# Eight experts on one core: all result stores behind the last weight load, smaller pieces of two weight matrices

## The chip, the cores and the metric

The kernel runs on one core of a Trainium2 chip. The other cores are idle. The metric is the device time of one launch in microseconds (us), as the median of three runs. A profile of one such launch is shorter by a little than the launch's own time, because it begins with the first instruction and ends with the last. Times "at 152.9 us" are counted from the start of that profiled span.

Five engines work side by side on a core: TensorE (PE, matrix products; its weight loads are listed as PEld), VectorE (DVE), ScalarE (ACT), GpSimd (POOL) and SyncE (SP). Data go between the chip's main memory (HBM) and the on-chip buffer (SBUF) by DMA. Three engines issue DMAs in this kernel. POOL issues all loads that convert fp32 to fp16 on the way, and most stores; the profile calls its queue q0. SP (q1) and ACT (q10) issue a few more.

## The reference

There are 8 experts. Each has 256 rows of input, a first layer from 512 to 2048 with a ReLU, and a second layer from 2048 to 512. All arrays are fp32.

```python
n_experts, capacity, hidden, expert_hidden = 8, 256, 512, 2048

def reference(x, w1, w2, b1, b2):
    h = np.matmul(x, w1) + b1[:, np.newaxis, :]
    h = np.maximum(h, 0)
    return (np.matmul(h, w2) + b2[:, np.newaxis, :]).astype(np.float32)
```

For each expert the first weights (w1) and the second weights (w2) are 4 MiB each in HBM, the input x and the result are 512 KiB each. So 8 experts read 64 MiB of weights and 4 MiB of x, and write 4 MiB of results.

## The kernel before

Weights are converted to fp16 while they are loaded, so a weight matrix fills 2 MiB of SBUF. All loads are issued on one queue, in an order that the program fixes (`ordered`). The list `ring` holds these issues, each with the step from which on it may be put out. `first_product(s)` computes the hidden layer of expert s, and `second_product(s - LAG)` the result of the expert three steps behind it.

```python
    LAG = 3
    LATE = (3, 4, 5, 6)
    PARTS = {5: ((0, 25, True), (25, 121, False), (121, 128, False))}
    nXF32 = 2
    ...
    w1_pool  = ... bufs=3
    w2_pool  = ... bufs=3
    w2t_pool = ... bufs=1          # the pieces of w2 of expert 7
    hT_pool  = ... bufs=LAG + 2    # hidden layers, 8 KiB per partition each
    out_pool = ... bufs=5          # results, 4 KiB per partition each
    ...
    def load_w2(e):
        src = w2[e].rearrange("(p j) h -> p j h", j=nJ)      # nJ = 16
        w2_sb[e] = []
        t = w2_pool.tile([P, nJ, H], fp16, tag="w2", name="w2sb")
        step = nJ if e < E - 2 else nJ // 2
        for lo in range(0, nJ, step):
            ordered(nc.gpsimd.dma_start(out=t[:, lo : lo + step, :], in_=src[:, lo : lo + step, :]))
            w2_sb[e].append((lo, lo + step, t[:, lo : lo + step, :]))

    def load_w2_piece(e, lo, hi):
        t = w2t_pool.tile([P, hi - lo, H], fp16, tag=f"w2_{lo}", name=f"w2_{lo}")
        ordered(nc.gpsimd.dma_start(out=t, in_=src[:, lo:hi, :]))
    ...
    def flush(e):                                            # the store of expert e, from POOL
        dst, src = pending.pop(e)
        for p0, p1, sync in PARTS.get(e, ((0, P, False),)):
            if not sync:
                ordered(nc.gpsimd.dma_start(out=dst[p0:p1], in_=src[p0:p1]))

    def store(e, po):
        out_sb = out_pool.tile([P, nTB, H], fp32, tag="out", name="out")
        nc.vector.tensor_copy(out=out_sb[:, 0, :], in_=po[0])
        nc.scalar.copy(out=out_sb[:, 1, :], in_=po[1])
        ...                                                  # e < 7: kept in pending for flush
        else:                                                # expert 7
            nc.sync.dma_start(out=dst[:, 0, :], in_=out_sb[:, 0, :])
            nc.scalar.dma_start(out=dst[:, 1, :], in_=out_sb[:, 1, :])

    def second_product(e):
        po = []
        for tb in range(nTB):                                # bias first
            ...matmul(out=t, lhsT=ones1, rhs=b2_sb[...], start=True, stop=False)
        for lo, hi, t in w2_sb[e]:                           # piece by piece
            for tb in range(nTB):
                for j in range(lo, hi):
                    ...matmul(out=po[tb], lhsT=hT[e][:, j, tb * P : (tb + 1) * P],
                              rhs=t[:, j - lo, :], start=False, stop=(j == nJ - 1))
        store(e, po)

    x32 = singles.tile([P, nXF32, nTB, H], fp32)             # x of experts 0 and 1 as fp32
    ...
    ring = []
    for s in range(1, E + LAG - 1):
        if s < E:
            if s >= nXF32:
                ring.append((s - 2, load_x, (s,)))
            ring.append((s - 2, load_w1, (s,)))
        if s >= LAG:
            ring.append((s - 2, load_w2, (s - LAG,)))
        if s >= 2 * LAG and s - 2 * LAG not in LATE:
            ring.append((s - 2, flush, (s - 2 * LAG,)))      # experts 0, 1, 2
    for lo, hi in ((0, 4), (4, 8), (8, 12), (12, 14), (14, 16)):
        ring.append((0, load_w2_piece, (E - 1, lo, hi)))
    for e in LATE:
        ring.append((e + LAG + 1, flush, (e,)))              # experts 3, 4, 5, 6

    for s in range(E + LAG):
        while ring and ring[0][0] <= s:
            _, put, args = ring.pop(0)
            put(*args)
        if s < E:
            first_product(s)
        if s >= LAG:
            second_product(s - LAG)
```

So the stores of experts 0, 1 and 2 stand among the loads: that of expert 0 between w2 of expert 3 and x of expert 6, that of expert 1 between w2 of expert 4 and w2 of expert 5, that of expert 2 between w2 of expert 5 and w2 of expert 6. The stores of experts 3 to 6 stand behind the last piece of w2 of expert 7. Expert 5's store is cut in three, of 25, 96 and 7 partitions; the first goes out from SP as soon as the result is there.

Of the kernel before, what the change touches and what calls it, by code (L numbers as in the profile page):

```python
# [11 lines left out]
def kernel(  # L12
# [9 lines left out]
    nc = tc.nc  # L22
    fp32 = mybir.dt.float32
    fp16 = mybir.dt.float16
    E, T, H = x.shape
    M = w1.shape[2]
    P = 128
    nTB = T // P
    nKC = H // P
    nJ = M // P  # L30
    LAG = 3
    LATE = (3, 4, 5, 6)

# [1 line left out]
    nXF32 = 2  # L37

    def ordered(ins):
        return tc.keep_in_program_order(ins)  # L40

    singles = ctx.enter_context(tc.tile_pool(name="singles", bufs=1))
# [2 lines left out]
    w2t_pool = ctx.enter_context(tc.tile_pool(name="w2t", bufs=1))  # L45
    x_pool = ctx.enter_context(tc.tile_pool(name="xp", bufs=4))
    xT_pool = ctx.enter_context(tc.tile_pool(name="xTp", bufs=2))
    hT_pool = ctx.enter_context(tc.tile_pool(name="hT", bufs=LAG + 2))
    out_pool = ctx.enter_context(tc.tile_pool(name="outp", bufs=5))
    psum_x = ctx.enter_context(tc.tile_pool(name="psum_x", bufs=1, space=bass.MemoryType.PSUM))  # L50
    psum_h = ctx.enter_context(tc.tile_pool(name="psum_h", bufs=3, space=bass.MemoryType.PSUM))
    psum_o = ctx.enter_context(tc.tile_pool(name="psum_o", bufs=2, space=bass.MemoryType.PSUM))
# [8 lines left out]
    x16 = [None] * E  # L61
# [3 lines left out]
    hT = [None] * E  # L65
# [14 lines left out]
    def load_w2(e):  # L80
        src = w2[e].rearrange("(p j) h -> p j h", j=nJ)
        w2_sb[e] = []
        t = w2_pool.tile([P, nJ, H], fp16, tag="w2", name="w2sb")
        step = nJ if e < E - 2 else nJ // 2
        for lo in range(0, nJ, step):
            ordered(nc.gpsimd.dma_start(out=t[:, lo : lo + step, :], in_=src[:, lo : lo + step, :]))  # L86
            w2_sb[e].append((lo, lo + step, t[:, lo : lo + step, :]))
# [80 lines left out]
                    ))  # L168
        store(e, po)

    x32 = singles.tile([P, nXF32, nTB, H], fp32)
    for e in range(nXF32):
        (nc.sync if e == 0 else nc.scalar).dma_start(out=x32[:, e], max_dma_last_dim=2048, in_=x[e].rearrange("(p tb) h -> p tb h", tb=nTB))
    nc.scalar.dma_start(out=b1_rows, in_=b1.rearrange("e (s i) -> (e s) i", s=2))
    load_w1(0)
    ordered(nc.gpsimd.dma_start(  # L176
        out=b2_sb,
        in_=b2.rearrange("e h -> (e h)").rearrange("(o f) -> o f", o=1),
# [4 lines left out]

    for e in range(nXF32):
        x16[e] = x_pool.tile([P, nTB, H], fp16, tag="x16", name="x16")
        nc.vector.tensor_copy(out=x16[e], in_=x32[:, e])  # L186

    pb = psum_x.tile([P, nJ, E, 2], fp32, tag="psx", name="pb")
    for j in range(nJ):
        for s in range(2):  # L190
            ordered(nc.tensor.matmul(  # L191
                out=pb[s * 64 : (s + 1) * 64, j, :, :],
# [5 lines left out]
    for s in range(2):  # L198
        nc.vector.tensor_copy(  # L199
            out=b1T[s * 64 : (s + 1) * 64, :, :], in_=pb[s * 64 : (s + 1) * 64, :, :, s]  # L200
# [5 lines left out]
# [5 lines that stand above are left out]
            ring.append((s - 2, load_w1, (s,)))  # L211
        if s >= LAG:
            ring.append((s - 2, load_w2, (s - LAG,)))
        if s >= 2 * LAG and s - 2 * LAG not in LATE:
            ring.append((s - 2, flush, (s - 2 * LAG,)))
    for lo, hi in ((0, 4), (4, 8), (8, 12), (12, 14), (14, 16)):
        ring.append((0, load_w2_piece, (E - 1, lo, hi)))
    for e in LATE:
        ring.append((e + LAG + 1, flush, (e,)))
# [40 lines left out]
```

## Time and profile before

| | |
|---|---|
| time, median of 3 runs | 183.32 us (182.97 to 183.61) |
| profiled span | 180.8 us |
| PE busy with matmuls | 138.1 us (76%) |
| ACT busy | 62.7 us (35%) |
| DVE busy | 13.2 us (7%) |
| POOL busy | 20.4 us (11%) |
| read from HBM, written to HBM | 71.39 MB, 4.19 MB |

The page gives busy times of the engines, the same in 40 slices of the span, the DMA queues, the chain of work that ended last, and the groups of instructions. Two things about its DMA figures help to read it. The GB/s of a slice count the bytes on the SBUF side, where a converted weight has half the size that it has in HBM: a store of fp32 results therefore shows about twice the GB/s of a weight load that keeps the DMA engines just as busy. And a DMA's time "from issue to landing" includes the time in which it stands behind earlier DMAs in its queue.

### The profile page before, as it was taken

The numbers are of one execution on the slowest core, as the hardware profiler recorded it, in microseconds if no ns is written. First come the engines' busy times: TensorE is split into PE (matmuls) and PEld (weight loads), VectorE is DVE, ScalarE is ACT, GpSimd is POOL, SyncE is SP. The second block draws the span as 40 slices with busy tenths as digits, with TensorE's granted clock in tenths as the row PEclk, the third lists the DMA queues.
The fourth block names the chain that finished last, engine by engine and source line by source line (L and its number), as shares of the span: only waits on it lengthen the run. The fifth ranks groups of instructions, "written<-read, shape, count | busy, mean of one in ns | idle before, by whom it ended". The sixth has DMA issues, their size and how long they took to land.

```text
span 180.8 us, 2129 instructions
## 1 busy us (share of the span) xinstructions
PE 138.1 (76%) x912; PEld 95.3 (53%) x912; DVE 13.2 (7%) x21; ACT 62.7 (35%) x137; POOL 20.4 (11%) x44
## 2 busy tenths in 40 slices
PE   0555979579550999939993799908999994999991
PEld 0544969469550754836473654807559641334340
DVE  0320001001000101010100101001010010010101
ACT  0022769639570340816044330903309501010101
POOL 7200030300300010210010100200004201112100
PEclk9999999969998599996999789996999999799999
DMA  5989999998999999899989999989998998999996
GB/s 187 281 185 234 232 199 207 204 260 174 234 232 207 199 232 232 177 229 232 225 181 226 238 210 196 228 234 233 232 225 181 290 228 241 223 209 218 213 367 243
DMA packets 5831, 40.58 MB, mean 224 GB/s; under 512 B 670, under 2 KB 686, under 8 KB 3774
## 3 DMA queue, kind: packets, MB, share of 16 engines
q0 software_dynamic: 4928, 38.71, 97.5%
q1 hardware_dynamic: 446, 0.89, 1.4%
q10 hardware_dynamic: 448, 0.85, 1.3%
q8 instruction: 7, 0.11, 0.2%
q14 instruction: 2, 0.02, 0.0%
HBM read 71.39 MB, written 4.19 MB: 418 GB/s over the span
## 4 chain that ended last, share of the span: by engine, by line
DMA 59%; PE 25%; issue 9%; another core or an unknown queue 3%; POOL 2%; ACT 0%; POOLq 0%; ACTq 0%
DMA x<-in_x_dram 25%; DMA w2sb<-in_w_dram 22%; PE po L162 16%; DMA w1sb<-in_w_dram 13%; PE ph L114 7%; PE po L156 1%; PE psx L101 1%; POOL w2sb L86 1%; POOL w1sb L76 1%; ACT out L140 0%; POOL out_dram L135 0%; POOL b_sb L176 0%; POOL ident masks.py:199 0%; POOL ident masks.py:197 0%
## 5 line engine op out<-in xcount | busy, mean ns | idle before, releaser
L114 PE MATMUL ph<-xT,w1sb 128*128 128x256 f16 x512 | 68.4, 300 | 9.8 <-DMA w1sb<-in_w_dram 9.8
L121 ACT ACTIVATE hT<-ph,b1T 128x256 f16<-128x256 f32 x128 | 57.1, 474 | 43.2 <-PE ph L114 42.8
L114 PEld LDWEIGHTS <-w1sb 128*128 128x128 f16 x512 | 61.5, 149 | 16.0 <-DMA w1sb<-in_w_dram 10.8
L162 PE MATMUL po<-w2sb,hT 128*128 128x512 f16 x224 | 51.2, 388 | 2.6 <-DMA w2sb<-in_w_dram 2.6
L162 PEld LDWEIGHTS <-hT 128*128 128x128 f16 x256 | 24.8, 99 | 35.6 <-issue 8.2
L140 ACT COPY out<-po 128x512 f32<-128x512 f32 x8 | 4.7, 588 | 60.6 <-PE po L162 60.6
L101 PE MATMUL psx<-ident,x 128*128 128x128 f16 x64 | 6.2, 254 | 19.7 <-DMA x<-in_x_dram 19.0
L101 PEld LDWEIGHTS <-x 128*128 128x128 f16 x64 | 5.0, 124 | 20.7 <-DMA x<-in_x_dram 19.9
L107 DVE COPY xT<-psx 128x1024 f16<-128x1024 f16 x8 | 5.5, 692 | 81.2 <-PE psx L101 81.2
L76 POOL DMA_DIRECT2D w1sb<-in_w_dram x8 | 4.5, 559 | 61.4 <-PE ph L114 60.6
L139 DVE COPY out<-po 128x512 f32<-128x512 f32 x8 | 5.5, 692 | 73.9 <-PE po L162 73.9
L86 POOL DMA_DIRECT2D w2sb<-in_w_dram x8 | 4.3, 534 | 48.2 <-PE po L162 48.2
L191 PE MATMUL pb<-ident,b_rows 16*64 16x16 f32 x64 | 3.7, 265 | 6.6 <-DMA b_rows<-in_b_dram 6.6
L162 PE MATMUL po<-w,hT 128*128 128x512 f16 x32 | 7.1, 379 | 0.0
L191 PEld LDWEIGHTS pb<-ident,b_rows 16*64 16x64 f32 x64 | 3.6, 198 | 6.5 <-issue 6.5
L135 POOL DMA_DIRECT2D out_dram<-out x8 | 4.3, 535 | 20.7 <-DMA w2sb<-in_w_dram 10.5
L121 ACT ACT_TABLE_LOAD x1 | 1.3, 1283 | 11.0 <-DVE b1T L199 11.0
L156 PE MATMUL po<-b_sb,ones 1*128 1x512 f16 x16 | 4.8, 379 | 0.0
L92 POOL DMA_DIRECT2D w<-in_w_dram x5 | 2.7, 540 | 14.4 <-DMA w2sb<-in_w_dram 13.7
L70 POOL DMA_DIRECT2D x<-in_x_dram x6 | 3.3, 548 | 5.3 <-DMA w2sb<-in_w_dram 4.6
L156 PEld LDWEIGHTS <-ones 1*128 1x128 f16 x16 | 0.9, 92 | 2.1 <-issue 2.1
L186 DVE CAST x<-x 128x1024 f16<-128x1024 f32 x2 | 1.4, 700 | 4.3 <-DMA x<-in_x_dram 4.3
(9 smaller groups left out, 2.6 us busy)
## 6 DMA issues: line engine op xcount, KB each, us to landing
w1sb<-in_w_dram POOLq DMA_DIRECT2D x8, 2048.0 KB, 33.7
w2sb<-in_w_dram POOLq DMA_DIRECT2D x6, 2048.0 KB, 45.3
out_dram<-out POOLq DMA_DIRECT2D x6, 512.0 KB, 30.1
w2sb<-in_w_dram POOLq DMA_DIRECT2D x2, 1024.0 KB, 25.6
x<-in_x_dram POOLq DMA_DIRECT2D x6, 256.0 KB, 38.9
w<-in_w_dram POOLq DMA_DIRECT2D x3, 512.0 KB, 29.7
x<-in_x_dram SPq DMA_DIRECT2D x1, 512.0 KB, 4.5
x<-in_x_dram ACTq DMA_DIRECT2D x1, 512.0 KB, 5.3
```

The source lines that it names most:

```text
L76: ordered(nc.gpsimd.dma_start(out=w1_sb[e], in_=w1[e].rearrange("(p kc) m -> p kc m", kc=nKC)))
L86: ordered(nc.gpsimd.dma_start(out=t[:, lo : lo + step, :], in_=src[:, lo : lo + step, :]))
L101: ordered(nc.tensor.transpose(out=pt[:, kc, tb * P : (tb + 1) * P], in_=x16[e][:, tb, :].rearrange("p (q kc) -> p q kc", kc=nKC)[:, :, kc] ...
L107: nc.vector.tensor_copy(out=xT[e], in_=pt)
L114: ordered(nc.tensor.matmul(out=ph, lhsT=w1_sb[e][:, kc, :].rearrange("p (q j) -> p q j", j=nJ)[:, :, j], rhs=xT[e][:, kc, :], start=(kc == 0),
L121: nc.scalar.activation(out=hT[e][:, j, :], in_=ph, func=mybir.ActivationFunctionType.Relu, bias=b1T[:, j, e : e + 1], scale=1.0,)
L135: ordered(nc.gpsimd.dma_start(out=dst[p0:p1], in_=src[p0:p1]))
L139: nc.vector.tensor_copy(out=out_sb[:, 0, :], in_=po[0])
L140: nc.scalar.copy(out=out_sb[:, 1, :], in_=po[1])
L156: ordered(nc.tensor.matmul(out=t, lhsT=ones1, rhs=b2_sb[0:1, e * H : (e + 1) * H], start=True, stop=False,))
L162: ordered(nc.tensor.matmul(out=po[tb], lhsT=hT[e][:, j, tb * P : (tb + 1) * P], rhs=t[:, j - lo, :], start=False, stop=(j == nJ - 1),))
L191: ordered(nc.tensor.matmul(out=pb[s * 64 : (s + 1) * 64, j, :, :], lhsT=b1_rows.rearrange("r (q j) -> r q j", j=nJ)[:, :, j], rhs=ident[0 ...
```

## The change

All seven stores of experts 0 to 6 are put behind the last load, so that no store stands in front of a weight. For that, all results have to be kept until then: eight result buffers in place of five. The room comes from the fp32 copies of x of experts 0 and 1, which now use two of these eight buffers (they are read once, at the start), and from the hidden layers, of which four are kept in place of five. Two loads are cut otherwise: w2 of expert 5 comes in two halves, so that its product can begin with the first half, and w2 of expert 7 in three pieces of 8, 4 and 4 rows in place of five of 4, 4, 4, 2 and 2.

```diff
-    LATE = (3, 4, 5, 6)
+    LATE = range(E - 1)
...
-    hT_pool = ctx.enter_context(tc.tile_pool(name="hT", bufs=LAG + 2))
-    out_pool = ctx.enter_context(tc.tile_pool(name="outp", bufs=5))
+    hT_pool = ctx.enter_context(tc.tile_pool(name="hT", bufs=LAG + 1))
+    out_pool = ctx.enter_context(tc.tile_pool(name="outp", bufs=E))
...
-        step = nJ if e < E - 2 else nJ // 2
+        step = nJ if e < E - 3 else nJ // 2
...
-    x32 = singles.tile([P, nXF32, nTB, H], fp32)
+    x32 = []
     for e in range(nXF32):
-        (nc.sync if e == 0 else nc.scalar).dma_start(out=x32[:, e], max_dma_last_dim=2048, in_=...)
+        x32.append(out_pool.tile([P, nTB, H], fp32, tag="out", name="x32"))
+        (nc.sync if e == 0 else nc.scalar).dma_start(out=x32[e], max_dma_last_dim=2048, in_=...)
...
-        if s >= 2 * LAG and s - 2 * LAG not in LATE:
-            ring.append((s - 2, flush, (s - 2 * LAG,)))
-    for lo, hi in ((0, 4), (4, 8), (8, 12), (12, 14), (14, 16)):
+    for lo, hi in ((0, 8), (8, 12), (12, 16)):
         ring.append((0, load_w2_piece, (E - 1, lo, hi)))
     for e in LATE:
         ring.append((e + LAG + 1, flush, (e,)))
```

One more thing moves by itself: ACT now issues the load of b1 ahead of its load of x of expert 1, where it was behind it.

More of the change, by code (lines that the diff above doesn't have):

```diff
@@ L169, in second_product @@
         store(e, po)
-    x32 = singles.tile([P, nXF32, nTB, H], fp32)
+    x32 = []
     for e in range(nXF32):
-        (nc.sync if e == 0 else nc.scalar).dma_start(out=x32[:, e], max_dma_last_dim=2048, in_=x[e].rearrange("(p tb) h -> p tb h", tb=nTB))
+        x32.append(out_pool.tile([P, nTB, H], fp32, tag="out", name="x32"))
+        (nc.sync if e == 0 else nc.scalar).dma_start(
+            out=x32[e], max_dma_last_dim=2048, in_=x[e].rearrange("(p tb) h -> p tb h", tb=nTB)
+        )
     nc.scalar.dma_start(out=b1_rows, in_=b1.rearrange("e (s i) -> (e s) i", s=2))
@@ L185 @@
         x16[e] = x_pool.tile([P, nTB, H], fp16, tag="x16", name="x16")
-        nc.vector.tensor_copy(out=x16[e], in_=x32[:, e])
+        nc.vector.tensor_copy(out=x16[e], in_=x32[e])
     pb = psum_x.tile([P, nJ, E, 2], fp32, tag="psx", name="pb")
```

## The prediction

> **What bounds the kernel now.** I read the DMA queues of the page first, because a kernel that moves 75 MB in 180 us is suspect there, then the slices, then the end of the span in short windows, and the chain of waits last.
>
> ```profile
> q0 software_dynamic: 4928, 38.71, 97.5%
> HBM read 71.39 MB, written 4.19 MB: 418 GB/s over the span
> DMA  5989999998999999899989999989998998999996
> GB/s 187 281 185 234 232 199 207 204 260 174 234 232 207 199 232 232 177 229 232 225 181 226 238 210 196 228 234 233 232 225 181 290 228 241 223 209 218 213 367 243
> ```
>
> POOL's queue alone keeps the 16 DMA engines occupied for 97.5% of the span; with q1 (1.4%), q10 (1.3%) and q8 (0.2%) it is 100.4%, so the records of packets overlap by a few per cent and no room is left. The DMA row is 8 or 9 in all slices but the first, some 2 us long at start-up, and the last. A single 8 is the resolution of the slices, since windows cut over the same time show a share of 1.00 or more. The windows are the view that carries the prediction (after the stretch come its length, then PE, PEld, DVE, ACT and POOL busy, the granted PE clock, the DMA share, GB/s on the SBUF side):
>
> ```profile
> 4.00:73.00 69.00, 49.15 (x398) 41.05 (x399) 6.13 (x10) 30.12 (x66) 6.77 (x13) 0.93 1.03 220
> 155.00:171.00 16.00, 16.00 (x71) 6.61 (x70) 1.38 (x2) 1.17 (x2) 2.42 (x5) 0.96 1.03 213
> 172.00:173.00 1.00, 1.00 (x6) 0.48 (x5) 0.00 (x0) 0.00 (x0) 0.00 (x0) 1.00 1.12 272
> 175.00:176.00 1.00, 1.00 (x7) 0.47 (x5) 0.00 (x0) 0.00 (x0) 0.00 (x0) 1.00 1.03 418
> 177.00:178.00 1.00, 0.00 (x0) 0.00 (x0) 0.09 (x1) 0.40 (x1) 0.00 (x0) 1.00 0.70 289
> 178.00:179.00 1.00, 0.00 (x0) 0.00 (x0) 0.00 (x0) 0.00 (x0) 0.00 (x0) 1.00 1.03 387
> 179.00:179.50 0.50, 0.00 (x0) 0.00 (x0) 0.00 (x0) 0.00 (x0) 0.00 (x0) 1.00 0.70 262
> 179.50:180.80 1.30, 0.00 (x0) 0.00 (x0) 0.00 (x0) 0.00 (x0) 0.00 (x0) 0.76 0.00 0
> ```
>
> The rate tells what moves: about 213 GB/s is weights (half size on this side), about 418 GB/s is results. The step between them lies in 172 to 173 us, so the last weight lands near 172.8. The DMA engines are full until 177, are at 0.70 for one microsecond (a loss of 0.30 us), work again until about 179.4, and 1.3 us later the span ends. All idle time that DMA has after the start is thus some 0.3 to 0.45 us at the end.
>
> PE, on the other hand, has slack, and waits for DMA at nearly every expert. Its last stretch:
>
> ```profile
> 122.62 1.04 PE L101 MATMUL psx<-ident,x 128*128 128x128 f16 x8 [5.33 <-DMA x<-in_x_dram]
> ...
> 149.72 0.60 PE L156 MATMUL po<-b_sb,ones 1*128 1x512 f16 x2
> 152.94 8.71 PE L162 MATMUL po<-w2sb,hT 128*128 128x512 f16 x32 [2.61 <-DMA w2sb<-in_w_dram]
> 161.57 0.60 PE L156 MATMUL po<-b_sb,ones 1*128 1x512 f16 x2
> 162.10 7.08 PE L162 MATMUL po<-w2sb,hT 128*128 128x512 f16 x32
> 169.12 0.60 PE L156 MATMUL po<-b_sb,ones 1*128 1x512 f16 x2
> 169.65 7.08 PE L162 MATMUL po<-w,hT 128*128 128x512 f16 x32
> ```
>
> The chain of waits goes back from expert 7's result through this stretch to w2 of expert 5 at 152.89. From there on it names PE, and that is the trap: PE is the last to wait, but at 176.75, when it ends, the queue still has results of the other experts to write until 178.
>
> **What the Trainium skill says.** "DMA: Bandwidth & Descriptors", section "Issuing engines are not separate DMA queues": DMAs of POOL, SP and ACT run on the same 16 engines and interleave. The trace agrees: the shares of the queues add up to the whole and no more. "Perfetto Trace Analysis", section "Roofline": one core alone is bounded by its 16 DMA engines at about 435 GB/s in all. Here 2 x 213 = 426 GB/s of weights on the HBM side and 418 GB/s of results come near it, in both directions. The same page, section "What 'DMA-bound' means", says that large descriptors matter then; the packet records of this trace agree in a small way. A packet of 16 rows of w2 (16 KiB) takes 1.227 us, one of 8 rows 0.625, of 4 rows 0.324, of 2 rows 0.173: some 0.02 us more for each cut.
>
> **The change, part by part.** Each store of 512 KiB takes 524,288 B / 418 GB/s = 1.25 us of all DMA engines, wherever it stands.
>
> 1. Stores of experts 0, 1, 2 moved: nothing is removed from DMA. x of expert 7 lands 1.25 us earlier (one store less before it), w2 of expert 5 2.5 us earlier, all later weights 3.75 us earlier. The last weight lands at 172.8 - 3.75 = 169.05.
>
> 2. Halves of w2 of expert 5: the first half lands a further 1,048,576 B / 213 GB/s = 4.9 us earlier, at 152.9 - 2.5 - 4.9 = 145.5, the second at 150.4. PE gets there at 149.72 + 0.55 - 1.25 = 149.0. So the wait of 2.61 us goes, and probably the slower product after it too (8.71 in place of 7.08, at a granted clock of 0.50 in 154 to 156 us). The product of expert 5 would end at 156.1.
>
> 3. PE to the end: bias 0.53, expert 6 until 163.6 (its halves land at about 154.3 and 159.2), bias, expert 7 from 164.15 (8 rows at 164.1, then 166.6 and 169.05). Each row takes PE 7.03 / 16 = 0.44 us; the last four rows can end at 171.2 at the earliest. PE's end moves from 176.75 to about 171.2 to 172.5, that is 4 to 5.5 us earlier. Result 7 is stored from SP and ACT right after, and these 512 KiB interleave with POOL's stores.
>
> 4. The DMA sum behind the last weight: seven results less the 25 partitions that SP stored before, 7 x 524,288 - 102,400 = 3.57 MB, and result 7, 0.52 MB: 4.09 MB / 418 GB/s = 9.8 us. 169.05 + 9.8 = 178.85. Before, DMA ended at 179.4. The difference is the idle stretch at 177 to 178, now filled, as PE no longer comes last: a gain of 0.3 to 0.45 us at most. The DMA engines do not all run out at the same instant, so the slowest one may have had no gap, and then this is 0. I take 0.3.
>
> 5. Cuts: w2 of expert 5 costs 8 packets per engine x (2 x 0.625 - 1.227) = +0.18 us; w2 of expert 7 had 3 x 0.324 + 2 x 0.173 = 1.318 per partition and has 0.625 + 2 x 0.324 = 1.273: 8 x -0.045 = -0.36. Together -0.18 us.
>
> 6. Buffers: four hidden layers are enough, since the first product of expert s needs the buffer that the second product of expert s - 4 has just left, and PE does these in this order anyway. Eight result buffers take two x and eight results; results 6 and 7 reuse those of x, free since 7 us. No wait on either. b1 before x of expert 1: PE's first product waits for w1 of expert 0 until 15.5 us in any case.
>
> Sum: -0.3 - 0.18, about -0.5 us on a DMA stream of 177 us. 183.32 - 0.5 = 182.8 us.
>
> **The rivals.**
> (a) PE sets the end, as the chain of waits has it. Then the 4 to 5.5 us of step 3 come out and the time is 178 to 179.3. For it: the chain's last 24 us are PE. Against it: the DMA share above. The bytes to write are the same, and 9.8 us of them now begin at 169.
> (b) The burst of stores is slower than 418 GB/s once it lasts 10 us and not 4. At 350 GB/s it would take 11.7 us in place of 9.8: time 184.7. For it: the trace shows pure stores for 4 us only. Against: within these, the rate doesn't fall (385, 426, 418, 397 from 173 to 177), and the packets of stores take 0.159 us both there and among the loads.
> (c) POOL issues too late and the queue runs dry. POOL waits for the landing of earlier DMAs before its last issues (9.1 us at most, before a piece of w2 of expert 7), as if eight could be under way at once. For it: each us that the queue is empty costs a us. Against: the queue is long. w2 of expert 6 was issued at 135.55, when work until 152.9 was before it; the longest median from issue to landing is 45.3 us. With three stores less among the loads it can only issue earlier. I expect no gap.
>
> **Range and chances.** The mechanism leaves little: between no gain (slowest engine had no gap, 183.3) and -0.7 us (all of step 4 and 5, 182.6), around which the runs scatter by 0.3 us. 182.1 to 183.5 should hold it 8 times in 10. 2% is 3.7 us, which only (a), or a strong form of (b) or (c), could bring: 2% faster, 2% slower, 96% within.
>
> **What would show it right or wrong.** Right: in the windows, the rate steps from about 213 to 418 GB/s near 169 us; DMA is full, without the dip to 0.70, until about 178.8; PE's wait of 2.61 us for w2 of expert 5 is gone and PE ends near 171.2 to 172.5; the chain of waits ends in stores, not in PE; the queue's share of the span stays near 97.5%. Wrong: a DMA share under 0.9 in any window of 2 us after the start (c), a rate under 400 GB/s behind the last load (b), or an end within 4 us after PE's (a). A result far below 182 would mean that the packets among the loads cost more in the mixture than the records show.

## The result, and the profile after

| | before | changed |
|---|---|---|
| time, median | 182.94 us (182.65 to 183.61) | 183.94 us (183.68 to 184.09) |
| ratio, 95% interval | | 1.0048 (1.0029 to 1.0068) |
| profiled span | 180.8 us | 181.9 us |

The changed kernel is half a per cent slower, about 1 us, where a gain of half a microsecond was predicted. (The 183.32 us from which the prediction started was the median of three runs; with six it is 182.94.) The page of the changed kernel shows the same full DMA queue; the share of POOL's queue fell from 97.5% to 96.5% because the span grew by 1.1 us and the queue's packets took 0.6 us less of each engine.

```profile
DMA  5999999999999999999999999899999999999993
GB/s 171 276 202 232 231 198 205 204 257 198 207 231 227 198 209 231 195 223 216 231 227 187 220 231 227 189 218 231 227 198 207 209 223 207 227 210 218 388 409 127
...
q0 software_dynamic: 4784, 38.71, 96.5%
...
HBM read 71.39 MB, written 4.19 MB: 415 GB/s over the span
```

The last three slices (4.5 us each) tell it already: full speed for two slices of stores, then a last slice at 3 tenths. The windows of the changed kernel, with the same columns as before, show where this comes from.

```profile
155.00:165.00 10.00, 10.00 (x47) 4.11 (x45) 1.38 (x2) 0.73 (x2) 1.06 (x2) 1.00 1.02 216
...
168.00:169.00 1.00, 1.00 (x7) 0.43 (x5) 0.00 (x0) 0.00 (x0) 0.10 (x1) 1.00 1.00 254
169.00:170.00 1.00, 1.00 (x6) 0.46 (x5) 0.00 (x0) 0.00 (x0) 0.00 (x0) 1.00 1.01 385
170.00:171.00 1.00, 1.00 (x6) 0.48 (x5) 0.00 (x0) 0.00 (x0) 0.55 (x1) 1.00 1.02 418
...
177.00:178.00 1.00, 0.00 (x0) 0.00 (x0) 0.00 (x0) 0.00 (x0) 0.00 (x0) 0.50 1.05 412
178.00:179.00 1.00, 0.00 (x0) 0.00 (x0) 0.00 (x0) 0.00 (x0) 0.00 (x0) 0.50 0.71 281
179.00:180.00 1.00, 0.00 (x0) 0.00 (x0) 0.00 (x0) 0.00 (x0) 0.00 (x0) 0.50 0.09 35
180.00:181.00 1.00, 0.00 (x0) 0.00 (x0) 0.00 (x0) 0.00 (x0) 0.00 (x0) 0.50 0.00 0
181.00:181.90 0.90, 0.00 (x0) 0.00 (x0) 0.00 (x0) 0.00 (x0) 0.00 (x0) 0.50 0.00 0
```

The rate steps up near 169, as worked out (the last packet of a weight ends at 169.45), and DMA is full until 178. On the average an engine runs out at 178 + 0.71 + 0.09 = 178.8. But they do not run out together: the last packet ends at 179.73. And then comes a stretch in which nothing moves at all: 2.2 us long, against 1.3 us before.

PE's last stretch, from the timeline of the changed kernel:

```profile
121.08 1.04 PE L101 MATMUL psx<-ident,x 128*128 128x128 f16 x8 [4.17 <-DMA x<-in_x_dram]
121.92 5.72 PE L114 MATMUL ph<-xT,w1sb 128*128 128x256 f16 x28
...
149.66 0.60 PE L156 MATMUL po<-b_sb,ones 1*128 1x512 f16 x2
150.19 7.08 PE L162 MATMUL po<-w2sb,hT 128*128 128x512 f16 x32
157.20 0.60 PE L156 MATMUL po<-b_sb,ones 1*128 1x512 f16 x2
157.74 7.08 PE L162 MATMUL po<-w2sb,hT 128*128 128x512 f16 x32
164.75 0.60 PE L156 MATMUL po<-b_sb,ones 1*128 1x512 f16 x2
165.28 7.08 PE L162 MATMUL po<-w,hT 128*128 128x512 f16 x32
```

The wait of 2.61 us is gone, the product of expert 5 takes 7.08 us and no longer 8.71, and PE ends at 172.4, 4.4 us earlier than before. None of it reaches the end.

What ends the span now is seen in the closing steps of the program. Each engine finishes with drains (the instruction DRAIN) and a few semaphore waits; the profile lists them under the line that calls the kernel. The columns are engine, operation, count, shortest, median and longest in ns, and the start of the first and of the last. The kernel before:

```profile
L255 POOLq DRAIN  x3: 46/107/9862, 170.1 to 180.5; - x3
L255 SPq DRAIN  x3: 7/7/7, 179.9 to 180.2; - x3
```

The changed kernel:

```profile
L256 POOLq DRAIN  x3: 46/107/10449, 170.7 to 181.6; - x3
L256 SPq DRAIN  x3: 7/7/7, 180.2 to 181.4; - x3
```

SP's first drain stands behind its wait for every store to land, so its start tells when SP is through: 179.9 before, 180.2 now. POOL's first drain after the start begins with its last issue and lasts until POOL's own queue is done and something more: 170.1 + 9.9 = 180.0 before, 170.7 + 10.4 = 181.1 now. Before, SP and POOL were through within 0.1 us of each other. Now POOL comes 0.9 us after SP, and the others wait for it. The packet records say what the drain follows. POOL's last packet ends at 178.12 before and at 179.33 now, and its drain ends 1.86 and 1.80 us later. SP needs only 0.4 us after the last packet of all (179.47 and 179.73). From the later of the two it is 0.8 us to the end of the span, in both.

So the theory ("drain"): a store on POOL's queue costs some 1.4 us (1.8 less 0.4) more than one on SP's or ACT's if it is the last to land. Before, result 7 came last from SP and ACT, its 1.25 us of DMA stood behind POOL's last packet, and POOL's drain lay beside it. The change lets PE end 4.4 us sooner, result 7 goes out beside POOL's stores and not behind them, POOL's last packet moves back by 1.21 us, and its drain sets the end. The rival ("uneven engines"): the end is late because some DMA engines have more to do than others, whoever issues.

### The profile page after: what moved, and what is told of

It reads as the page before. It is cut to its first block, busy times and chain, and to the rows that moved or that the text cites. A ratio compares the mean times of both kernels' runs of the same rounds, so it can differ in the third digit from the quotient of the medians.

```text
span 181.9 us, 2120 instructions
## 1 busy us (share of the span) xinstructions
PE 137.1 (75%) x912; PEld 95.6 (53%) x912; DVE 13.2 (7%) x21; ACT 62.6 (34%) x137; POOL 20.0 (11%) x43
## 3 DMA queue, kind: packets, MB, share of 16 engines
q0 software_dynamic: 4784, 38.71, 96.5%
## 4 chain that ended last, share of the span: by engine, by line
DMA 52%; PE 41%; issue 1%; POOL 1%; ACT 0%; POOLq 0%
DMA x<-in_x_dram 44%; PE po L162 23%; PE ph L114 15%; DMA w1sb<-in_w_dram 8%; PE po L156 2%; PE psx L101 1%; POOL w2sb L86 0%; ACT out L140 0%; POOL w1sb L76 0%; POOLq L245 0%
## 5 line engine op out<-in xcount | busy, mean ns | idle before, releaser
L162 PE MATMUL po<-w2sb,hT 128*128 128x512 f16 x224 | 49.6, 379 | 0.0
L101 PE MATMUL psx<-ident,x 128*128 128x128 f16 x64 | 7.0, 276 | 19.8 <-DMA x<-in_x_dram 19.1
L101 PEld LDWEIGHTS <-x 128*128 128x128 f16 x64 | 5.6, 131 | 20.9 <-DMA x<-in_x_dram 20.1
L86 POOL DMA_DIRECT2D w2sb<-in_w_dram x9 | 4.8, 536 | 55.2 <-PE po L162 55.2
L92 POOL DMA_DIRECT2D w<-in_w_dram x3 | 1.6, 557 | 0.0
```

What stands on the lines that cost most here:

```text
L101: ordered(nc.tensor.transpose(out=pt[:, kc, tb * P : (tb + 1) * P], in_=x16[e][:, tb, :].rearrange("p (q kc) -> p q kc", kc=nKC)[:, :, kc] ...
L162: ordered(nc.tensor.matmul(out=po[tb], lhsT=hT[e][:, j, tb * P : (tb + 1) * P], rhs=t[:, j - lo, :], start=False, stop=(j == nJ - 1),))
```

## The experiments

In all of them the time is compared with the kernel before in runs on the same chip (medians of 182.9 to 183.0); the ratio is to it, with its 95% interval. Differences between two changed kernels are differences of their medians.

**The last store from another queue, in the kernel before.** The smallest test: half of result 7, the same bytes in the same place.

```diff
-            nc.scalar.dma_start(out=dst[:, 1, :], in_=out_sb[:, 1, :])
+            nc.gpsimd.dma_start(out=dst[:, 1, :], in_=out_sb[:, 1, :])
```

> The kernel before, but half of the result of expert 7 is stored from POOL and not from ACT. The same bytes at the same place of the end, only the queue differs. Theory (drain): POOL's last packet is then at about 179.4 and its drain ends 1.8 us later, where SP was through 0.5 us after its last packet: 1.1 to 1.4 us slower than before, 184.1 to 184.3. Rival (uneven engines): who issues makes no difference: 182.9 within 0.3.

184.39 us, ratio 1.0085 (1.0068 to 1.0103): 1.45 us slower, a little more than the 1.1 to 1.4 us expected. The closing steps of that run:

```profile
L255 POOLq DRAIN  x3: 46/98/5268, 176.1 to 181.9; - x3
L255 SPq DRAIN  x3: 7/7/7, 180.3 to 181.7; - x3
```

POOL's drain ends at 176.1 + 5.3 = 181.4, SP is through at 180.3. POOL's last packet is at 179.50: 1.9 us before the end of the drain. The cost of the queue alone is shown, in a kernel without the change.

**The parts of the change apart.**

```diff
 late_only: stores and buffers as changed, but
-    for lo, hi in ((0, 8), (8, 12), (12, 16)):
+    for lo, hi in ((0, 4), (4, 8), (8, 12), (12, 14), (14, 16)):
-        step = nJ if e < E - 3 else nJ // 2
+        step = nJ if e < E - 2 else nJ // 2
 pieces_only: the kernel before with these two lines as changed
```

> Only the move of the stores and its buffers, with the weight pieces as before the change. Theory (drain): the whole loss comes from the stores of POOL's queue now being the last packets, so it is all here: 1.0 to 1.3 us above the kernel before, 0.2 of that from smaller pieces of w2 of expert 7. Rival (pieces): if the new cuts are what costs, this one is at the time of before, 182.9 within 0.3.

> The kernel before with nothing but the new cuts of w2 of experts 5 and 7; the stores stay where they were. The packet records say 0.18 us less DMA work, and PE loses its wait of 2.6 us for w2 of expert 5. Theory (drain): result 7 then comes earlier, goes out beside POOL's last stores, POOL's queue is the last to end and its drain sets the end: part of the loss comes back, 0.3 to 1.0 us above before. Rival (DMA work alone counts): 0.2 us below before, 182.7.

The stores alone: 183.96 us, 1.0062 (1.005 to 1.0074). The whole loss is there. The drain ends 1.1 us after SP is through. The pieces alone: 182.81 us, 0.9991 (0.9982 to 1.0), 0.1 below the kernel before and near the 182.7 of the rival, DMA work alone. The loss that I expected of the drain here didn't come: result 7 was still the last to land (179.78, POOL's last packet 178.49), and POOL and SP were through at the same time, as before the change. That also says how narrow the border is: PE ended at 176.3 there, only 0.5 us sooner than before, as it waited for the later weights instead.

**Expert 5's store uncut.**

```diff
-    PARTS = {5: ((0, 25, True), (25, 121, False), (121, 128, False))}
+    PARTS = {}
```

> The changed kernel, but the store of expert 5 is not cut in 25, 96 and 7 partitions; POOL stores it whole. Rival (uneven engines): the cut gives a few DMA engines 0.8 us more than the others, and without it all run out together, near 178.9: the last packet 0.6 us or more earlier, time 183.3 or below. If the cut evens out an unevenness from elsewhere, the spread grows and the time rises by as much. Theory (drain): the time follows POOL's last packet, by whatever this moves, and POOL's drain still ends last, some 0.9 us after SP: 183.9 within 0.3.

184.25 us, 1.0077 (1.0064 to 1.009), 0.3 above the changed kernel. The last packet of SP and ACT comes 1.1 us earlier (178.64) but POOL's 0.2 us later (179.53), and the end follows POOL: its drain ends at 181.3, SP is through at 180.1. So a last packet 1 us earlier on the queue that doesn't end the span is worth nothing. The profiled span also has a gap of 0.37 us in the close, taken up below.

**Store 6 from SP, as soon as it is there.**

```diff
-    PARTS = {5: ((0, 25, True), (25, 121, False), (121, 128, False))}
+    PARTS = {5: ((0, 25, True), (25, 121, False), (121, 128, False)), 6: ((0, 128, True),)}
```

> The changed kernel, but the store of expert 6 goes out from SP instead of POOL. It lands among the last loads, so POOL's last packets are those of expert 5. Theory (drain): the changed kernel ends with POOL's closing drain, which lasts until about 1.8 us after the last packet of POOL's queue; SP is through with its own waits 0.9 us sooner. With POOL's last packet over 1 us earlier the drain ends before SP, and the time falls by about 0.9 us, from 183.9 to 183.0. Rival (uneven engines): the end is late because some DMA engines run out at 179.7 and others at 178.5; a store of 128 partitions loads all alike whoever issues it, so nothing changes: 183.9 within 0.2.

184.5 us, 1.0091 (1.0076 to 1.0105): 0.6 slower than the changed kernel, not 0.9 faster. Neither theory had this, and the fault is in my expectation. SP issued its store at 165, its packets ran at 168 to 171 among the last loads and POOL's first late stores, and the last packet of a weight ended at 170.08 in place of 169.45. POOL's queue lost a store and yet its last packet came at 179.50, 0.17 us later. The drain followed it as always:

```profile
L256 POOLq DRAIN  x3: 40/168/13594, 167.7 to 182.2; - x3
L256 SPq DRAIN  x3: 7/7/7, 180.1 to 181.9; - x3
```

167.7 + 13.6 = 181.3, 1.1 us after SP. With a full DMA it isn't enough to take a store off a queue: it has to come after that queue's last one.

**Stores behind result 7, from SP.** This is the same idea put right. SP is made to issue the late stores behind the store of result 7, so that they run when POOL's queue is already empty.

```diff
+    TAIL = (4, 5, 6)            # in a second run (6,)
-    LATE = range(E - 1)
+    LATE = [e for e in range(E - 1) if e not in TAIL]
-    PARTS = {5: ((0, 25, True), (25, 121, False), (121, 128, False))}
+    PARTS = {}
-            nc.sync.dma_start(out=dst[:, 0, :], in_=out_sb[:, 0, :])
+            ordered(nc.sync.dma_start(out=dst[:, 0, :], in_=out_sb[:, 0, :]))
             nc.scalar.dma_start(out=dst[:, 1, :], in_=out_sb[:, 1, :])
+            for k in TAIL:
+                d, o = pending.pop(k)
+                ordered(nc.sync.dma_start(out=d, in_=o))
```

> The changed kernel, but results 4, 5 and 6 (uncut) are stored from SP behind the result of expert 7, so that POOL keeps only the stores 0 to 3 and its queue runs empty near 176, while SP's stores run to the end. The same bytes, the same place behind the loads. Theory (drain): POOL's closing drain ends 1.8 us after its last packet, near 178, long before SP; SP ends the span 1.3 us after the last packet of all, near 179.0: span 180.2 to 180.4, time 182.3, 1.6 below the changed kernel and 0.6 below the one before. Rival (uneven engines): the DMA engines have the same bytes and the last packet stays at 179.5 or later, and the end with it: 183.6 to 183.9.

> As the run with results 4, 5 and 6 behind the result of expert 7, but with result 6 alone there; POOL keeps 0 to 5 (5 uncut). Theory (drain): POOL's queue has some 3.6 us of stores left when SP begins at 173, shares the engines with SP and ends at 178.3 to 178.9; its drain is over 1.8 us later and the span 0.75 us after that: 180.9 to 181.4, time 182.9 to 183.5, between the two. Rival (uneven engines): as for the other, 183.6 to 183.9.

With 4, 5 and 6 on SP: 182.98 us, 1.0007 (0.9996 to 1.0018). That is 1.0 below the changed kernel, with the same loads and the same bytes; less than the 1.6 expected. With 6 alone: 183.52 us, 1.003 (1.002 to 1.0039), between the two, as the theory has it. Nearest to both is the run with store 5 uncut (184.25), which cuts the stores alike and has the gap in its close too: the three stores are worth 1.3 us against it, the one 0.7. The closing steps, first of the run with three stores on SP:

```profile
L260 POOLq EVENT_SEMAPHORE  x4: 17/17/17, 180.0 to 181.0; - x4
L260 POOLq DRAIN  x3: 51/108/20432, 155.7 to 180.5; - x3
L260 SPq DRAIN  x3: 7/7/7, 179.9 to 180.2; - x3
```

and of the run with one:

```profile
L260 POOLq DRAIN  x3: 45/231/15021, 165.4 to 181.4; - x3
L260 SPq DRAIN  x3: 7/7/7, 179.9 to 180.7; - x3
```

With three stores moved POOL's drain is over at 155.7 + 20.4 = 176.1 and SP alone ends the span. With one it ends at 180.4, again 1.75 us behind POOL's last packet (178.69) and 0.5 us behind SP.

What was missing of the 1.6 us is in two places. The first is the rival's point: in the windows of the run with three stores on SP

```profile
176.00:178.00 2.00, 0.00 (x0) 0.00 (x0) 0.00 (x0) 0.00 (x0) 0.00 (x0) 0.50 1.04 424
178.00:178.50 0.50, 0.00 (x0) 0.00 (x0) 0.00 (x0) 0.00 (x0) 0.00 (x0) 0.50 0.81 328
178.50:179.00 0.50, 0.00 (x0) 0.00 (x0) 0.00 (x0) 0.00 (x0) 0.00 (x0) 0.50 0.46 188
179.00:179.50 0.50, 0.00 (x0) 0.00 (x0) 0.00 (x0) 0.00 (x0) 0.00 (x0) 0.50 0.31 123
```

DMA falls off in two steps. By the packet records nine of the sixteen completions of SP's last store, which I read as one for each engine, come at 178.3 to 178.7 and seven at 179.4 to 179.5. The last packet is at 179.5 and not at the 179.0 that I had taken from equal shares. The second is the line of POOL's semaphore steps: the first starts at 180.0 and the last at 181.0, where in the kernel before it is 180.0 to 180.7. Most of the difference is one gap of 0.38 us, ahead of the last of these steps.

**The gap in the close.** It was there, 0.36 to 0.38 us long, in four of the runs whose POOL program is shorter than the changed kernel's (76 recorded POOL instructions): with store 5 uncut (75), store 6 from SP (74), one store behind result 7 (73) and three (69). It sat at another step each time: with one instruction less one step later, and with four less four steps later. It always stands ahead of the 69th recorded POOL instruction. So it seemed to belong to a place in POOL's program and not to a step.

```diff
+    pad = singles.tile([P, 16], fp32, name="pad")
     for s in range(E + LAG):
+        if s == 2:
+            for i in range(16):
+                ordered(nc.gpsimd.memset(pad[:, i : i + 1], 0.0))
```

> As the run with results 4, 5 and 6 on SP, plus 16 memsets of one column of an unused tile on POOL, early, where POOL waits anyway. In that run the closing sequence had a gap of 0.39 us between two of POOL's last steps; in the other runs with a shorter POOL program it sits at the same place of POOL's program and so at another step of the close. Theory (place in the program): with 16 instructions more this place comes long before the end, where POOL waits for data, and the close is 0.4 us shorter: 182.6. Rival (the gap belongs to the close or to SP's stores): 183.0 as before.

182.57 us, 0.9977 (0.997 to 0.9984). 0.41 below the same kernel without the memsets, as the theory asked for, and the fastest of all: 0.4 us below the kernel before, 1.4 below the changed one. In its close POOL's semaphore steps stand closer again:

```profile
L264 POOLq EVENT_SEMAPHORE  x4: 17/17/17, 180.1 to 180.7; - x4
L264 SPq DRAIN  x3: 7/7/7, 180.0 to 180.3; - x3
```

The Trainium skill ("Runtime: NRT & Kernel Launch", section "Instruction fetch mechanics") says that an engine's program is fetched in blocks of 16 KiB and that crossing from one to the next is mostly hidden. A fetch fits what was seen, a stall at one place of a program. The packet records support it in part: wherever a 69th POOL instruction is recorded, a packet of kind instruction on q14, of 8 KiB and not 16, starts 0.7 to 3.4 us after it begins. That is at 174.1 in the changed kernel and at 140.3 with the memsets; in the runs with the gap it is at 181.7 to 182.7, some 0.7 to 1.0 us behind the gap. So that packet isn't what POOL waited for, and that it waited for a fetch at all was not shown. The gap is as large as the 0.3 us by which the run with store 5 uncut came out above the changed kernel, and over half of the 0.6 us of the run with store 6 from SP; in the changed kernel this place lies ahead of the drain, where POOL waits in any case.

**The uneven engines.**

```diff
+    CUT = {6: ((0, 27), (27, 123), (123, 128))}
             for k in TAIL:
                 d, o = pending.pop(k)
-                ordered(nc.sync.dma_start(out=d, in_=o))
+                for p0, p1 in CUT.get(k, ((0, P),)):
+                    ordered(nc.sync.dma_start(out=d[p0:p1], in_=o[p0:p1]))
```

> As the run with results 4, 5 and 6 on SP, but result 6, the last of all, is cut in 27, 96 and 5 partitions. There 9 of the 16 DMA engines were done at 178.3 to 178.7 and 7 at 179.4 to 179.5. The cut is meant to give up to nine engines 3 or 4 packets of 0.16 us more than the rest. Theory (uneven engines matter, once POOL's drain is off the end): if those nine are the early ones, all end near 178.9 and the time falls by 0.4 to 0.5 us, to 182.5; if they are the late ones, the last packet comes 0.3 us later and the time rises by as much. Rival (only the drain counts): 183.0, no change.

> Both: the memsets and the cut. If the two effects are separate they add up: 182.1 to 182.2 where the cut helps, 0.7 to 0.8 us below the kernel before; 182.9 where it hurts.

183.56 us, 1.0038 (1.0024 to 1.0052), and with the memsets 183.16 us, 1.0014 (1.0007 to 1.002): 0.6 slower than without the cut in both, which also says that the two effects add up. The cut did even out the engines: 15 of 16 completions now fall in 178.7 to 179.25, in place of two groups. But one came at 179.65, so the last packet was no earlier, and SP, with two more stores to wait for, was through 0.85 us after it and no longer 0.43; that the two stores cause this was not tested apart. The cut cost more than it gave. Which engines are the loaded ones, and by what, is open; seven fetches on q8 of 0.9 us each in the packet records would fit the seven late engines, but no run tested it.

**w2 of expert 5 in one piece again**, with 4, 5 and 6 on SP:

```diff
-        step = nJ if e < E - 3 else nJ // 2
+        step = nJ if e < E - 2 else nJ // 2
```

> As the run with results 4, 5 and 6 on SP, but w2 of expert 5 is loaded in one piece as before the change. By the packet records this saves 0.18 us of every DMA engine, and PE waits some 1.3 us for it, which is off the path if DMA sets the end: 0.1 to 0.2 us below that run. Rival (PE still matters): PE's end moves 1.3 to 3 us later, SP's stores with it, DMA runs dry before they come, and it is over 1 us slower than that run.

183.03 us, 1.0018 (1.0006 to 1.003), in the median level with the run that has the halves (182.98). But its 22 runs fall in two groups, 14 at 182.90 to 183.06 us and 8 at 183.67 to 183.89, and the profile is of one of the longer ones (183.89). Its windows:

```profile
172.00:174.00 2.00, 2.00 (x11) 0.78 (x8) 0.65 (x1) 0.00 (x0) 0.00 (x0) 1.00 0.84 342
174.00:176.00 2.00, 0.18 (x1) 0.00 (x0) 0.04 (x1) 0.58 (x1) 0.00 (x0) 1.00 0.64 246
```

PE waits 2.1 us for the whole matrix and ends 2.2 us later, at 174.2. POOL's four stores are nearly over by then and SP's wait behind result 7, so DMA is idle for 1.0 us (0.16 and 0.36 of 2 us each), and the last packet comes 0.85 us later than with the halves. So the rival's mechanism is in the trace, and in 8 of 22 runs some 0.8 us of it is in the time. What the other 14 do, whose span is some 180.7 us and not 181.5, no profile shows. The gain of 0.1 to 0.2 us that I expected isn't there.

The gap needs care here. POOL's program is one instruction shorter again (68), and its recorded close has no gap. But the time of a launch exceeds its span by 2.3 us in all 22 runs, against 1.7 to 1.9 us in the runs of the other kernels: some 0.5 us lie outside the span, which fits a gap that has only moved to where the 69th would be. What the halves are worth alone stays open.

One thing more: after the idle stretch all sixteen completions of SP's last store came at 180.17 to 180.34, and the two groups were gone. That fits late engines that were behind with their work and caught up while DMA was idle.

## Why the prediction was wrong

Steps 1 to 3 held. The last weight lands near 169, the wait and the slow product are gone, and PE ends at 172.4, inside the stretch given. Only PE's course before it was off by a microsecond: the product after x of expert 7 took 5.72 us, at a mean granted clock of 0.55, in place of 4.25 us at 0.75, so PE reached expert 5 at 150.2 and not at 149.0.

Step 5 held: the packets of the profiled execution add up to 181.3 us for each engine, 181.6 before. Step 6 held too: nothing waits on one of the buffers that were changed.

Rival (a) was rightly put aside: 4.4 us of PE came to nothing. Rival (b) fell: the burst holds 385 to 426 GB/s for nine microseconds. Rival (c) fell: no gap in DMA before 177. The sign set for it, a share under 0.9 in a window of 2 us, could not tell: such windows show 0.61 to 1.37 in both kernels, low ones beside high ones. The packet records can, and between 6 and 177 us they have at least 16 packets under way at every moment.

The step that failed is the fourth. Its sum of bytes is right, and the average engine does run out at 178.8, against 178.85 predicted. Two things it took over from the kernel before without asking:

- "1.3 us later the span ends". That was the close behind SP and ACT. Behind POOL's last packet there stand 1.8 us of drain and 0.8 us of close. The closing steps of the kernel before had it, POOL's drain of 9.9 us that ends level with SP, but the prediction read the page and the windows, which do not show them. Measured: 2.2 us, 0.9 more.
- That the last packet comes when the average one does. I had named the doubt, and counted it as a gain of 0 at worst. It comes 0.9 us later, at 179.73, and so 0.26 us later than before. The dip that was to be filled was no gap for all: in the kernel before, at least nine packets were under way at every moment of 177 to 178.

Together 1.8 us: 178.85 + 1.3 = 180.15 by the step, 179.73 + 2.2 = 181.9 measured. (The sum took only 0.3 of the 0.6 us that the step put the end earlier, so the forecast time was off by less.) Without POOL's drain and with the same close, SP's side would have ended at 180.2 + 0.8 = 181.0, so the drain is 0.9 of the 1.1 us by which the span grew, and the last packet the rest. The runs show the drain from both sides: half a result moved to POOL's queue costs 1.45 us in the kernel before, three stores moved behind POOL's last give back 1.0 us in the changed one, and one gives back 0.4.

The prediction also expected the chain of waits to end in stores. It doesn't: in the changed kernel it ends with ACT's copy of result 7 at 173.0 and says nothing of the last 9 us. Where DMAs run on after the last instruction of the compute engines, that view stops too early, and the windows and the closing steps have to be read.

## What to carry to other kernels

Where DMA is full from beginning to end, moving transfers about changes only who is last, so ask which queue's last packet ends the program and what that queue needs after it. Here POOL's needed 1.4 us more than SP's, and letting result 7 go out earlier, which looks like a gain, put POOL last. In such a kernel, try the last stores on SP or ACT, behind the ones on POOL in time and not only on another queue; and before a gain of some tenths is believed, read the closing steps of each engine, as a gap of 0.4 us can come and go there with the length of a program.

## What the runs showed of the hardware

- POOL's closing drain ended 1.6 to 1.9 us after the last packet of POOL's queue in all runs, whether this packet was among the last of all (1.91, half of result 7 from POOL) or the drain was over long before the end (1.61, w2 of expert 5 whole). SP was through 0.4 to 0.9 us after the last packet of all queues.
- A gap of 0.36 to 0.38 us stood in POOL's close, always ahead of the 69th recorded POOL instruction; 16 memsets took it away (-0.41 us). With 68 recorded instructions the profiled span had no such gap, but the time exceeded the span by 2.3 us in place of 1.7 to 1.9.
- With three stores behind result 7, seven of the sixteen completions of SP's last store came at 179.4 to 179.5, a microsecond behind most of the other nine; with w2 of expert 5 whole, after an idle microsecond of DMA, all sixteen came within 0.2 us. What had put the seven behind is open.
